# Moving SyncE's jump to its next instruction block from the exit into its idle time before the last store

## Chip, cores and metric

One core of one Trainium2 chip. The metric is the device time of one execution in microseconds (us). Executions are compared as medians of several runs. The profile of one execution has a span of its own, from the first to the last recorded instruction of the program; the device time is about 1.8 us longer than it (1248.58 against 1246.8 for the profiled run before). All times "at 1243.9" are us from the start of the profiled span. Besides the printed views, I use the raw records behind them, which have every instruction with its start and length in ns, every semaphore signal and every DMA packet; tables of SyncE's instructions that are not profile views hold numbers taken from these records.

## The reference

```python
x: (64, 256, 8192) float32
out = np.mean(x, axis=2)          # (64, 256)
```

537 MB are read once and 64 KB are written.

## The kernel before

The 16384 rows are read in 63 blocks of 256 rows (8 MB each) into three buffers. VectorE sums each block. The last 256 rows come in seven smaller loads, so that little is left to do when the last bytes land: row 0 of each partition as one load, row 1 in six chunks of 4096 to 256 columns. SyncE issues all loads and all three stores.

```python
FETCH_BLOCK = 128
LAST_CHUNKS = (4096, 2048, 1024, 512, 256, 256)
# ...
tail_sem = [tc.alloc_semaphore(f"tail{i}") for i in range(len(LAST_CHUNKS) + 1)]

nc.vector.addr_align(FETCH_BLOCK, offset=0, max_nops=0)     # VectorE: at its start, both kernels
# ...
def store_last(r):
    nc.vector.transpose(out=fin_t[r][:], in_=fin[r][:])
    nc.sync.dma_start(out=out_last[r], in_=fin_t[r][0:P:SQ, :])

for n in range(LB):                                   # LB = 63
    xt = slots[n % SLOTS]
    load(xt[:], x_v[n], load_sem[n % LOAD_SEMS])      # issued by SyncE
    # ... VectorE sums it (the last one together with ScalarE)

# ... row 0 of the rest: one load; row 1: one load per chunk, each with its own semaphore;
# ... each but the last is summed by VectorE (the wide ones together with ScalarE)

nc.sync.dma_start(out=out_bulk, in_=bulk[:LB])        # means of the 63 blocks

scaled_sum(fin[0][:, 0:1], head[:])
store_last(0)                                         # row 0
untracked(scaled_sum(fin[1][:, 0:1], fin_in[:, 0 : lastw + k]))._wait_ge(sem, 16)
store_last(1)                                         # row 1: the last store
```

`addr_align(128, max_nops=0)` asks for the next instruction of that engine to be placed at the start of a block of 128 instruction slots, without filling instructions. The trace does not number the slots; it shows the align as one COMPARE_BRANCH (VectorE's at 0.762, 47 ns).

The framework adds the exit, the code that ends every kernel. On SyncE it is three semaphore waits (a semaphore counts signals, in the trace 16 for each load; each of the waits is for one of the three stores, merged with another wait), a drain (DRAIN in the trace), a second drain that signals the barrier, at which each of the five engines waits for the other four (before: SyncE's signal, the last, at 1246.070, and the engines' next instructions between 1246.094 and 1246.226), and the rest of the barrier.

## Time and profile before

| | before |
|---|---|
| device time, median of 3 (lowest to highest) | 1248.35 us (1248.23 to 1248.42) |
| span of the profiled run | 1246.8 us |
| HBM traffic over the span | 431 GB/s |
| last load chunk landed / last store landed | 1242.87 / 1245.43 |
| from the last store's landing to the end of the span | 1.376 us |

From the page of the kernel before: the span, the share of busy DMA and the rate in 40 slices, the DMA queues, and the largest group of instructions (busy us, mean ns | idle us before it and what ended it).

```profile
span 1246.8 us, 224 instructions
...
DMA  9999999999999999999999999999999999999998
GB/s 404 437 437 437 435 431 418 431 437 437 437 437 437 435 433 418 429 437 437 437 437 437 435 431 414 435 437 437 437 437 435 437 429 416 435 437 437 437 437 339
...
q1 hardware_dynamic: 10168, 536.94, 99.6%
q14 instruction: 1, 0.01, 0.0%
...
L95 DVE TENSOR_REDUCE res<-xt 128x2 f32<-128x16384 f32 (+1 forms) x63 | 1076.4, 17086 | 154.0 <-DMA xt<-in_x_dram 154.0
```

The kernel is bound by its loads. DMA is busy nine tenths or more everywhere but in the last slice, and VectorE idles almost only for loads (154.0 us). Queue 14 carries instructions: one packet of 8192 bytes inside the span, at 4.88, 4.1 us after VectorE's jump at 0.76.

The change concerns the last 4 us. The timeline of the kernel before, cut to its end (start us, length us, engine, line, operation):

```profile
1243.19 0.43 DVE L101 TENSOR_SCALAR_CACHE_REDUCE fin_in<-fin_in 128x265 f32<-128x265 f32 x1 [0.15 <-DVE fin_in L95]
1243.55 0.08 DVE L101 DVE_READ_ACCUMULATOR fin_in<-fin_in 128x1 f32 x1
1243.66 0.21 DVE L112 STREAM_TRANSPOSE fin_t<-fin 128x32 f32<-128x32 f32 x1
1243.90 0.50 SPq L113 DMA_DIRECT2D out_dram<-fin_t  x1
```

The timeline ends here, 2.4 us before the span does, because drains and semaphore waits are not counted as work. The view of the exit's source line (L187), cut to the end of the span, has them (duration ns min/median/max, first and last start us):

```profile
L187 SPq EVENT_SEMAPHORE  x5: 17/28/28, 1244.5 to 1246.7; - x5
L187 POOLq EVENT_SEMAPHORE  x4: 17/17/17, 1246.1 to 1246.7; - x4
L187 SPq DRAIN  x3: 7/7/114, 1245.5 to 1246.3; - x3
```

Two of SyncE's drains take 7 ns and one takes 114. The raw records of SyncE show where it stands and what is around it:

```
before           start     ns
last store     1243.902   502   landed 1245.432
wait           1244.450    28
wait           1244.525    28
wait           1245.449    28   (for the last store's landing)
drain          1245.519     7
drain          1245.954   114   signals the barrier at 1246.070
...
end            1246.808
instruction packet, 8192 bytes, at 1246.869
```

Between the starts of the two drains lie 0.435 us; elsewhere in this exit, where nothing has to be awaited, SyncE needs 0.07 to 0.09 us from the start of one instruction to the start of the next. The other four engines had joined the barrier by 1243.93, so everybody waits for this.

### The profile page before, as it was taken

What the parts mean: (1) busy time and instruction counts of PE and PEld (TensorE: products, weight loads), DVE (VectorE), ACT (ScalarE), POOL (GpSimd) and SP (SyncE); (2) the same over time, 40 slices, a digit from 0 to 9 for tenths busy, and PEclk for the clock granted to TensorE, in tenths of its full rate; (3) what the DMA queues carried; (4) which work ended last, traced back from release to release, by engine and by line L of the source; (5) the groups of instructions that cost most, each with busy time, mean ns of one, the idle gap of its engine ahead of it and who ended that gap; (6) DMA issues with size and microseconds to landing.
All of it is one profiled execution on the core that took longest, in us unless ns stands there. A gap on an engine that the chain in (4) does not pass through costs nothing.

```text
span 1246.8 us, 224 instructions
## 1 busy us (share of the span) xinstructions
PE 0.9 (0%) x2; PEld 0.4 (0%) x2; DVE 1087.3 (87%) x79; ACT 16.5 (1%) x13; POOL 0.7 (0%) x6
## 2 busy tenths in 40 slices
PE   0000000000000000000000000000000000000000
PEld 0000000000000000000000000000000000000000
DVE  2898988989889889898898988989889888898897
ACT  0000000000000000000000000000000000000004
POOL 0000000000000000000000000000000000000000
DMA  9999999999999999999999999999999999999998
GB/s 404 437 437 437 435 431 418 431 437 437 437 437 437 435 433 418 429 437 437 437 437 437 435 431 414 435 437 437 437 437 435 437 429 416 435 437 437 437 437 339
DMA packets 10169, 536.95 MB, mean 431 GB/s; under 512 B 1145, under 2 KB 1464, under 8 KB 1720
## 3 DMA queue, kind: packets, MB, share of 16 engines
q1 hardware_dynamic: 10168, 536.94, 99.6%
q14 instruction: 1, 0.01, 0.0%
HBM read 536.87 MB, written 0.07 MB: 431 GB/s over the span
## 4 chain that ended last, share of the span: by engine, by line
DMA 70%; DVE 29%; SPq 0%; issue 0%; DVEq 0%
DMA xt<-in_x_dram 70%; DVE res L95 29%; DVE fin_in L95 0%; SPq L85 0%; DVE fin_in L101 0%; DVE fin_t L112 0%; DVEq L101 0%
## 5 line engine op out<-in xcount | busy, mean ns | idle before, releaser
L95 DVE TENSOR_REDUCE res<-xt 128x2 f32<-128x16384 f32 (+1 forms) x63 | 1076.4, 17086 | 154.0 <-DMA xt<-in_x_dram 154.0
L98 ACT ACT_TABLE_LOAD x1 | 1.3, 1283 | 1182.5 <-DVE res L95 1182.5
L98 ACT ACTIVATE xt<-xt 128x8192 f32<-128x8192 f32 (+5 forms) x6 | 14.7, 2443 | 43.9 <-DMA xt<-in_x_dram 43.7
L95 DVE TENSOR_REDUCE fin_in<-xt 128x1 f32<-128x256 f32 (+3 forms) x5 | 4.9, 1003 | 0.3 <-DMA xt<-in_x_dram 0.2
L95 DVE TENSOR_REDUCE head<-xt 128x1 f32<-128x4096 f32 x1 | 4.4, 4420 | 0.2 <-DMA xt<-in_x_dram 0.2
L154 PE MATMUL ps<-ident,res 128*63 128x128 f32 x2 | 0.9, 458 | 1231.5 <-ACT xt L98 1230.4
L75 DVE MEMSET fin<- 128x32 f32 x2 | 0.1, 85 | 1.4 <-PEq L176 1.4
L98 ACT ACTIVATION_READ_ACCUMULATOR xt<-xt 128x1 f32 x6 | 1.1, 186 | 0.0
L155 DVE TENSOR_SCALAR bulk<-ps 63x128 f32<-63x128 f32 x2 | 0.6, 278 | 0.4 <-PE ps L154 0.4
L154 PEld LDWEIGHTS ps<-ident,res 128*63 128x63 f32 x2 | 0.4, 180 | 1231.8 <-issue 1230.4
L101 DVE TENSOR_SCALAR_CACHE_REDUCE fin_in<-fin_in 128x265 f32<-128x265 f32 x1 | 0.4, 431 | 0.2 <-DVE fin_in L95 0.2
L112 DVE STREAM_TRANSPOSE fin_t<-fin 128x32 f32<-128x32 f32 x2 | 0.4, 211 | 0.1
L63 POOL TENSOR_SCALAR_AFFINE_SELECT ident<-ident 128x128 f32<-128x128 f32 x1 | 0.3, 292 | 0.1
L101 DVE TENSOR_SCALAR_CACHE_REDUCE head<-head 128x2 f32<-128x2 f32 x1 | 0.2, 155 | 0.1
L62 POOL MEMSET ident<- 128x128 f32 x1 | 0.2, 204 | 0.3 <-POOLq L176 0.3
L176 POOL MEMSET const-bfloat16-1.0<- 128x1 bf16 x1 | 0.1, 101 | 0.0
L176 POOL MEMSET const-uint8-127<- 128x1 uint8 x1 | 0.1, 101 | 0.0
L176 POOL MEMSET const-float32-0.0<- 128x1 f32 x1 | 0.1, 98 | 0.2 <-issue 0.2
L176 POOL MEMSET const-float32-1.0<- 128x1 f32 x1 | 0.1, 98 | 0.0
L101 DVE DVE_READ_ACCUMULATOR head<-head 128x1 f32 x1 | 0.1, 83 | 0.0
L101 DVE DVE_READ_ACCUMULATOR fin_in<-fin_in 128x1 f32 x1 | 0.1, 83 | 0.0
## 6 DMA issues: line engine op xcount, KB each, us to landing
xt<-in_x_dram SPq DMA_DIRECT2D x1, 4096.0 KB, 31.1
xt<-in_x_dram SPq DMA_DIRECT2D x1, 2048.0 KB, 35.7
xt<-in_x_dram SPq DMA_DIRECT2D x1, 1024.0 KB, 37.7
xt<-in_x_dram SPq DMA_DIRECT2D x63, 40.8
xt<-in_x_dram SPq DMA_DIRECT2D x1, 512.0 KB, 38.5
xt<-in_x_dram SPq DMA_DIRECT2D x1, 256.0 KB, 38.7
xt<-in_x_dram SPq DMA_DIRECT2D x1, 128.0 KB, 38.5
fin_in<-in_x_dram SPq DMA_DIRECT2D x1, 128.0 KB, 38.4
```

The lines of the kernel that those rows point to most:

```text
L62: nc.gpsimd.memset(ident[:], 0.0)
L63: nc.gpsimd.affine_select(out=ident[:], in_=ident[:], compare_op=mybir.AluOpType.not_equal, fill=1.0, base=0, pattern=[[-1, P]], channel_m ...
L75: nc.vector.memset(fin[r][:], 0.0)
L95: return untracked(nc.vector.tensor_reduce(out=dst, in_=src, axis=X, op=ADD))
L98: return untracked(nc.scalar.activation(out=src, in_=src, func=COPY, accum_out=dst))
L101: return nc.vector.tensor_scalar(out=src, in0=src, scalar1=inv, scalar2=None, op0=mybir.AluOpType.mult, op1=ADD, accum_out=dst,)
L112: nc.vector.transpose(out=fin_t[r][:], in_=fin[r][:])
L154: nc.tensor.transpose(out=ps[:LB, :], in_=res[:, r, :], identity=ident[:])
L155: nc.vector.tensor_scalar_mul(out=bulk[:LB, :, r], in0=ps[:LB, :], scalar1=inv)
L176: nc = _bacc.Bacc("TRN2", target_bir_lowering=False, num_devices=1)
```

## The change

Its intent: I read the hole of 0.435 us as SyncE coming to the end of a block of its instructions in the middle of the exit. It shall go to the next block earlier, at a time when it has nothing to do: after the second-last chunk has landed, while VectorE computes the last sums.

```diff
     def store_last(r):
         nc.vector.transpose(out=fin_t[r][:], in_=fin[r][:])
-        nc.sync.dma_start(out=out_last[r], in_=fin_t[r][0:P:SQ, :])
+        return nc.sync.dma_start(out=out_last[r], in_=fin_t[r][0:P:SQ, :])
@@
     scaled_sum(fin[0][:, 0:1], head[:])
-    store_last(0)
+    st = store_last(0)
+
+    with tc.issue_after(st.ins):
+        st = nc.sync.wait_ge(tail_sem[-2], 16)
+    with tc.issue_after(st.ins):
+        st = nc.sync.addr_align(FETCH_BLOCK, offset=0, max_nops=0)
     untracked(scaled_sum(fin[1][:, 0:1], fin_in[:, 0 : lastw + k]))._wait_ge(sem, 16)
-    store_last(1)
+    with tc.issue_after(st.ins):
+        store_last(1)
```

A comparison of the two built programs shows one instruction more on SyncE (the wait is merged into the align) and the same order on all other engines.

## The prediction

The sum below comes to minus 0.40 us, 1248.35 to 1247.95 us.

> **What bounds the kernel now.** It reads 537 MB once; the page gives 431 GB/s over the 1246.8 us span and DMA nine tenths or more busy in 39 of 40 slices. VectorE (1087 us) waits for loads alone (154 us). The change touches no load and no reduction; it can act only on the last microseconds.

> **The tail, from the raw records of the trace (us from the span's start).** The second-last load chunk has landed at 1242.58, the last at 1242.87. VectorE's last transpose signals at 1243.89. SyncE issues the last store at 1243.90 (0.50 us); it lands at 1245.43. SyncE then passes three semaphore waits (to 1245.48) and a drain (1245.519 to 1245.526). Its next instruction, the drain that joins the exit barrier, starts only at 1245.954 and takes 0.114 us. Elsewhere in this exit SyncE takes 0.07 to 0.09 us from one instruction's start to the next, and its other two drains take 0.007 us (view of the exit's source line). SyncE's waits show this hole as a 0.5 us wait put down to PE, which had long been done. All other engines had joined by 1243.93, so the hole is wholly on the critical path.

> I read it as SyncE stepping into its next instruction block: an 8192-byte packet on the instruction queue follows at 1246.87, 1.3 us later, as one follows VectorE's own jump at 0.76 (at 4.88, behind the first loads). As the fetch comes after the step, the block stepped into was already on the core. [...] this trace shows 8 KiB packets.

> **What the change does.** It adds one SyncE instruction, an align to a 128-instruction block with the wait for the second-last chunk merged into it; nothing moves on the other engines (order compared). SyncE is idle between 1238.55 and 1243.90. The jump starts near 1242.6. VectorE's identical one took some 0.55 us (0.76 to about 1.3), so SyncE is ready at about 1243.2, 0.7 us before the last store is released: off the critical path. Its block fetch (0.31 us on one engine) should run near 1244, between the loads' end (1242.87) and the store's packets (1245.05).

> **Sum.** The hole of 0.435 us between two drains' starts becomes 0.07: minus 0.37. The drain's 0.114 may become 0.01; I count a third of that. About minus 0.40 us: 1248.35 becomes **1247.95 us**, 0.03% less, twice the spread of the runs before (0.19 us). Range for 8 in 10: **1247.70 to 1248.40**. Chances: faster by over 2% 0.002, within 2% 0.996, slower by over 2% 0.002.

> **What would show it right.** SyncE's barrier drain follows the drain before it within 0.1 us; from the store's landing to the span's end falls from 1.37 us to about 0.97; two instruction-queue packets inside the span instead of one; a compare-branch on SyncE near 1242.6; the last store still issues within 0.03 us of the transpose's signal.

> **What would make it wrong.** The target block is not on the core: the jump waits for a fetch, the last store issues late, and the time rises by up to a microsecond. Or the hole is no block step but belongs to the first drain, and stays. Or the fetch collides with the store's packets or descriptors and delays its landing by 0.3 us. Or the shifted code crosses another block after the exit, at the same cost.

## The result

| | before | after |
|---|---|---|
| device time, median of 6 runs (lowest to highest) | 1248.43 us (1248.23 to 1248.86) | 1247.91 us (1247.77 to 1248.15) |
| span of the profiled run | 1246.8 us | 1246.4 us |
| last load chunk landed | 1242.872 | 1242.943 |
| transpose's signal to the last store's issue | 0.016 us | 0.017 us |
| last store's landing to the end of the span | 1.376 us | 0.898 us |

The ratio is 0.9996, with a 95% interval of 0.9983 to 1.0009. Ratios are computed as the mean time of one kernel's runs over that of the other's of the same rounds, so not quite the ratio of the medians quoted. By that interval the kernels are the same within 2%, and it does not by itself exclude no gain. But the slowest run after (1248.15) is faster than the fastest before (1248.23), and the profile shows where the difference lies. Three of the six runs before are those of the first table, and the lines on the tail before come from the profile taken then.

The page after:

```profile
span 1246.4 us, 226 instructions
...
q1 hardware_dynamic: 10168, 536.94, 99.7%
q14 instruction: 2, 0.02, 0.0%
```

There are two packets of instructions in the span instead of one. The timeline after, cut to its end:

```profile
1243.22 0.43 DVE L101 TENSOR_SCALAR_CACHE_REDUCE fin_in<-fin_in 128x265 f32<-128x265 f32 x1 [0.15 <-DVE fin_in L95]
1243.57 0.08 DVE L101 DVE_READ_ACCUMULATOR fin_in<-fin_in 128x1 f32 x1
1243.69 0.21 DVE L112 STREAM_TRANSPOSE fin_t<-fin 128x32 f32<-128x32 f32 x1
1243.93 0.51 SPq L113 DMA_DIRECT2D out_dram<-fin_t  x1
```

The last store follows the transpose as closely as before, so SyncE was back from its jump in time. The views of the align's source line (L164) and of the exit's (now L193):

```profile
L164 SPq NOP  x1: 14/14/14, 1242.6 to 1242.6; - x1
L164 SPq COMPARE_BRANCH  x1: 32/32/32, 1242.7 to 1242.7; - x1
```

```profile
L193 SPq EVENT_SEMAPHORE  x5: 17/28/28, 1244.5 to 1246.3; - x5
L193 SPq DRAIN  x3: 7/7/13, 1245.6 to 1245.9; - x3
```

The drain of 114 ns is gone. In the raw records the hole is gone too:

```
after            start     ns
NOP (the wait) 1242.635    14
COMPARE_BRANCH 1242.697    32
instruction packet, 8192 bytes, at 1243.726, 539 ns
last store     1243.931   512   landed 1245.477
wait           1245.493    28
drain          1245.558    13
drain          1245.628     7   signals the barrier at 1245.637
end            1246.375
```

From the first drain's start to the signal it takes 0.079 us instead of 0.551, which is 0.472 us less. From the store's landing to the end it is 0.478 us less. The device time fell by 0.52 us in the medians. The part ahead of the store's landing varies by some tenths from one execution to the next (the last chunk landed 0.07 us later in the profile after, and between 1242.75 and 1243.15 over all nine profiles), so the stretch after the landing is the cleaner measure, and the table of the experiments uses it.

One of my readings of the profile was wrong. The waits of SyncE before had these lines, of which I took the second for the hole:

```profile
SPq L187 <- DMA out_dram<-fin_t: 0.9, 1, 0.9
SPq L187 <- PEq L187: 0.6, 2, 0.5
```

Both are still there after the change:

```profile
SPq L193 <- DMA out_dram<-fin_t: 0.9, 1, 0.9
...
SPq L193 <- PEq L193: 0.6, 2, 0.5
```

So the second line is something else: SyncE's last wait in the barrier, which begins 0.43 us after the drain ahead of it has ended (1246.313 to 1246.746 before, 1245.880 to 1246.313 after), while GpSimd clears the semaphores (EVENT_SEMAPHORE_RANGE_CLEAR, 142 ns, at 1246.377 before and 1245.943 after). The hole itself is in no view of waits, because SyncE waited for no semaphore in it. Only the starts and lengths of the exit's instructions show it.

### The profile page after: what moved, and what is told of

It is laid out like the page before. It is cut to its first block, busy times and chain, and to the rows that moved or that the text cites. A ratio compares the mean times of both kernels' runs of the same rounds, so it can differ in the third digit from the quotient of the medians.

```text
span 1246.4 us, 226 instructions
## 1 busy us (share of the span) xinstructions
PE 0.9 (0%) x2; PEld 0.4 (0%) x2; DVE 1087.3 (87%) x79; ACT 16.4 (1%) x13; POOL 0.7 (0%) x6
## 4 chain that ended last, share of the span: by engine, by line
DMA 70%; DVE 29%; SPq 0%; issue 0%; DVEq 0%
DMA xt<-in_x_dram 70%; DVE res L95 29%; DVE fin_in L95 0%; SPq L85 0%; DVE fin_in L101 0%; DVE fin_t L112 0%; DVEq L101 0%
```

## The experiments

| run | device time, median (before in the same rounds) | store landed to end of span, us | place of the step |
|---|---|---|---|
| before | 1248.43 (first comparison) | 1.376 | between the drains |
| after | 1247.91 (1248.43) | 0.898 | branch at 1242.7 |
| after_again | 1248.09 (1248.54) | 0.899 | branch at 1242.6 |
| wait_only | 1248.53 (1248.54) | 1.419 | ahead of the first drain |
| shift2 | 1248.03 (1248.54) | 0.930 | among the waits (estimate), no branch |
| late | 1248.17 (1248.54) | 0.898 | branch at 1244.5 |
| early | 1248.11 (1248.45) | 0.893 | branch at 1238.5 |
| twojumps | 1249.46 (1248.45) | 0.887 | branches at 1242.5 and 1243.1 |
| dve_cross | 1248.04 (1248.45) | 0.892 | as after; VectorE's align removed |

Five runs of each, nine of before in each of the two sets (after_again to late on one chip; early, twojumps and dve_cross on another). All gave correct results.

### after_again: the changed kernel beside the others

> The changed kernel again, on the chip of the runs beside it. Both theories expect about 0.5 us less than before (1248.43 to 1247.91 in the first comparison), a compare-branch on SyncE within 0.1 us after the second-last chunk has landed, and no hole at the exit: from the start of SyncE's first exit drain to its signal to the barrier about 0.08 us instead of 0.55.

The branch starts at 1242.641, after the second-last chunk's landing at 1242.563. From the first drain's start (1245.496) to the signal (1245.574) it takes 0.078 us. The medians differ by 0.45 us. The result repeats.

### wait_only: the wait without the align

```diff
     with tc.issue_after(st.ins):
         st = nc.sync.wait_ge(tail_sem[-2], 16)
-    with tc.issue_after(st.ins):
-        st = nc.sync.addr_align(FETCH_BLOCK, offset=0, max_nops=0)
```

> The added wait is kept, the align is taken out: SyncE has one instruction more in the stream, and no jump. Theory (a step into the next block, at a fixed place in the stream): the step now falls one instruction earlier in the exit, ahead of the first exit drain instead of after it, still after the store has landed (1245.4). So the hole of about 0.4 us stays but moves from after that drain to before it; time as before within 0.15 us; one instruction packet inside the span. Rival (the hole belongs to the barrier drain itself, or comes from SyncE having slept since 1238.6 and the added wait wakes it): under the first form the hole stays after the first drain; under the second it is gone and the time falls by 0.5 us as in the changed kernel.

The time is that of before (1248.53 against 1248.54). The exit's drains, in the view of its source line, and the raw records:

```profile
L191 SPq DRAIN  x3: 7/7/112, 1245.8 to 1246.3; - x3
```

```
wait_only        start     ns
wait           1245.358    28
drain          1245.834   112
drain          1246.013     7
```

The long drain is now the first of the three, not the second. The hole moved with it: 0.476 us from the last wait's start to the drain's, where it is 0.065 after the change. So the hole and the slow instruction behind it belong to a place in the stream of instructions and not to a certain drain, and one instruction more shifted them by one. Waking SyncE gains nothing. Both rivals of that kind fall. Only my count of instruction packets was off: the fetch came at 1246.46, just inside the span, so the page counts two.

### shift2: two more instructions and no jump

```diff
-        st = nc.sync.wait_ge(tail_sem[-2], 16)
-    with tc.issue_after(st.ins):
-        st = nc.sync.addr_align(FETCH_BLOCK, offset=0, max_nops=0)
+        st = nc.sync.wait_ge(tail_sem[0], 16)
+    # ... likewise tail_sem[1], tail_sem[2], tail_sem[3]; the four become two instructions
```

> No jump and no align: two wait instructions on chunks that have landed or are about to are put in SyncE's idle time, so everything after them stands two places later. Theory: the step falls between the second and the third semaphore wait of the exit, in the time (1244.55 to 1245.43) in which SyncE waits for the last store to land anyway. It is hidden there: time about 0.45 to 0.5 us below before, equal to the changed kernel within 0.15 us, with no hole among the drains, an instruction packet near 1245.6 to 1245.9 and no compare-branch on SyncE. Rival (the jump itself, or the early fetch, is what helps): no gain, or the hole stays.

The median is 0.51 us below before and 0.06 from the changed kernel's. The drains are quick:

```profile
L197 SPq DRAIN  x3: 7/7/7, 1245.8 to 1246.1; - x3
```

There is no branch on SyncE. The instruction packet comes at 1246.13, somewhat later than I had expected. The place of a hidden step can only be told from its packet. Apart from the run early and the second jump of twojumps, the packet came 1.03 to 1.34 us after SyncE's branch, or after the end of the instruction ahead of the hole, in every profile where that place is known (before: 1245.526 to 1246.869). Reckoned back from 1246.13, that puts the step here, as an estimate, between 1244.79 and 1245.10: after the second wait of the exit, which ends at 1244.786, and well before the store lands at 1245.674. By this estimate the step fell where it was meant to, in the time in which SyncE waits for the store to land. From the landing to the end it takes 0.930 us, 0.03 more than after; this difference lies between the third wait and the first drain (0.099 against 0.065). The branch is not what helps: this shift takes the step off the critical path without one and does the same.

### late: the jump while the store is under way

```diff
-    with tc.issue_after(st.ins):
-        st = nc.sync.wait_ge(tail_sem[-2], 16)
-    with tc.issue_after(st.ins):
-        st = nc.sync.addr_align(FETCH_BLOCK, offset=0, max_nops=0)
 ...
-    with tc.issue_after(st.ins):
-        store_last(1)
+    st = store_last(1)
+    with tc.issue_after(st.ins):
+        nc.sync.addr_align(FETCH_BLOCK, offset=0, max_nops=0)
```

> The align is put after the last store's issue, without a wait, so SyncE jumps at about 1244.45 while the store is under way (landing at about 1245.43). Theory: the jump's 0.5 to 0.6 us end at about 1245.0, before the landing, so it is hidden just as well: about 0.45 us below before, equal to the changed kernel within 0.15 us; the instruction packet runs near 1245.5. Rival (the jump has to come while the sums run, ahead of the last store): gain lost or at most half of it.

The branch starts at 1244.502 and the exit's first wait at 1244.964, so the jump takes 0.46 us. The store lands at 1245.491, and from there to the end it is 0.898 us, exactly as in the changed kernel. The median is 0.37 us below before, with runs from 1247.82 to 1248.54: a little less than I had expected, but the profile has nothing left of the hole, and a difference of 0.08 us to the changed kernel beside it is within the spread of either. The jump need not come while the sums run.

### early: the jump without the wait

```diff
     with tc.issue_after(st.ins):
-        st = nc.sync.wait_ge(tail_sem[-2], 16)
-    with tc.issue_after(st.ins):
         st = nc.sync.addr_align(FETCH_BLOCK, offset=0, max_nops=0)
```

> The changed kernel without its wait: SyncE jumps as soon as the first of the two short stores is issued (1238.6), so the block fetch runs near 1239.7, while loads still stream to 1242.9. The hole at the exit stays away, as in the changed kernel (store's landing to the end 0.90 us). If the fetch takes its 0.3 to 0.5 us from the one queue engine that finishes the loads last, the last chunk lands up to 0.3 to 0.5 us later and most of the gain is lost; if it falls to any other engine the time equals the changed kernel's within 0.15 us. There the wait for the second-last chunk is only a precaution.

The branch runs at 1238.541, but the instruction packet only at 1241.602, 3.06 us later, where the changed kernel needed 1.03. There the last load had landed 0.78 us before the packet ran; here, as at VectorE's packet at the start (4.1 us after its jump), loads were under way. What held these two packets back was not shown. The packet runs before the loads are done, and yet the last chunk landed at 1242.804, no later than in the other profiles (1242.75 to 1243.15), and the last of its 16 completion signals was 0.60 us behind the one before it, against 0.77 in the last chunk that landed before the fetch. No delay of the loads shows. The exit is as good (0.893 us). The median is 0.34 us below before, against 0.45 and 0.52 for the changed kernel in other rounds and 0.41 for dve_cross, which has the wait, in the same rounds. So the wait was worth about 0.1 us or nothing; five runs do not settle which.

### twojumps: a second jump right behind the first

```diff
     with tc.issue_after(st.ins):
         st = nc.sync.addr_align(FETCH_BLOCK, offset=0, max_nops=0)
+    # ... three satisfied waits on tail_sem[0], [1], [2]
+    with tc.issue_after(st.ins):
+        st = nc.sync.addr_align(FETCH_BLOCK, offset=0, max_nops=0)
```

> The changed kernel with a second align after the first, two satisfied waits between them, so that SyncE jumps twice: into the block that is on the core, and from there at once into the one behind it, whose fetch only the first jump sets off (it ran from 1.05 us after the branch, for 0.5 us). If a block that is not on the core has to be awaited, the second jump, near 1243.1, ends only after that fetch has landed near 1244.2, the last store issues 0.4 to 1.0 us late, and the time is 0.4 to 1.0 us above the changed kernel, that is at or above the time before. If two blocks ahead are already held, the second jump ends near 1243.6, in time for the store at 1243.9, and the time equals the changed kernel's within 0.15 us.

The expectation spoke of two waits between the aligns. There are three in the program; in the trace two of them are one instruction, and the third is merged into the second align. The timeline of this run, cut to its end:

```profile
1243.51 0.21 DVE L112 STREAM_TRANSPOSE fin_t<-fin 128x32 f32<-128x32 f32 x1
1245.31 0.52 SPq L113 DMA_DIRECT2D out_dram<-fin_t  x1
```

The store issues 1.58 us after the transpose's signal (1243.733 to 1245.309), although it waited for no other semaphore. The first branch took 0.451 us (1242.521 to the next instruction at 1242.972); the second took 2.18 us (1243.127 to 1245.309). The time is 1.01 us above before and so about 1.5 us above the changed kernel. The direction is as the expectation has it for a block that is not on the core: SyncE goes on only after the packet that followed the first jump, 2.79 us after that jump. The size was more than I had expected (0.4 to 1.0 us). The packet ran from 1243.798 to 1244.122, and SyncE went on 1.19 us after that. What it did in this time no record shows. When SyncE has gone on, the next packet follows at 1245.887.

This is the failure that the prediction named first. The changed kernel has one jump alone; such a first jump took 0.45 us here and 0.46 in late, and not 2.18, and here SyncE went on from it 0.83 us before the packet ran. So what it went on with was already on the core.

### dve_cross: VectorE without its align

```diff
-    nc.vector.addr_align(FETCH_BLOCK, offset=0, max_nops=0)
```

> The changed kernel without the align at VectorE's start, which both kernels have. The theory that a step into the next block sits at a fixed place in each engine's stream, if VectorE starts its stream about where SyncE does, puts VectorE's step some 4 instructions ahead of its last drain: a hole of about 0.4 us at the last wait, the last sum or the last transpose, on the critical path. Against that, no fetch of VectorE runs at 5 us among the first loads, so if that fetch sets one DMA engine 0.31 us behind for good, the last chunk lands up to 0.3 us earlier. Sum: 0.1 to 0.5 us above the changed kernel. If there is no hole on VectorE and no earlier landing, the time equals the changed kernel's.

My expectation was wrong in its place: VectorE does not step just ahead of its last drain, so by the theory it does not start its stream where SyncE does. There is no hole in the tail, and the time equals the changed kernel's (0.41 us below before). The branch of VectorE and the packet near 5 us are gone. In their place one packet runs in the middle of the run, so I take it that VectorE's step is now there; no hole of VectorE shows it, as VectorE waits for a load before each sum (2.13 to 2.84 us in these lines). The timeline there (in brackets: VectorE's idle time before the instruction):

```profile
816.21 17.22 DVE L94 TENSOR_REDUCE res<-xt 128x2 f32<-128x16384 f32 x1 [2.13 <-DMA xt<-in_x_dram]
835.55 17.22 DVE L94 TENSOR_REDUCE res<-xt 128x2 f32<-128x16384 f32 x1 [2.13 <-DMA xt<-in_x_dram]
855.62 17.22 DVE L94 TENSOR_REDUCE res<-xt 128x2 f32<-128x16384 f32 x1 [2.84 <-DMA xt<-in_x_dram]
874.96 17.22 DVE L94 TENSOR_REDUCE res<-xt 128x2 f32<-128x16384 f32 x1 [2.13 <-DMA xt<-in_x_dram]
```

The only instruction packet among the loads runs at 839.638, for 0.33 us. The next block lands 0.71 us late, once. In the raw records each load ends with 16 signals. Up to that packet the last of them comes about 0.13 us after the one before it, and from then on, for the 400 us to the end, about 0.7 us after it. With the align at the start the first load bears this instead: it lands at 22.67 here and at 23.12 to 23.44 in the other profiles. So at both of these places one fetch of 8 KB set the loads behind it back by 0.45 to 0.77 us. It is no rule for every place: in early a fetch ran at 1241.602 among the last loads and the last chunk was not late. Both kernels have VectorE's fetch among the loads once (at 4.88 before, 5.08 after). SyncE's fetch holds up no load in either, since it comes after the last one (at 1246.869 against 1242.872 before, 1243.726 against 1242.943 after).

This run also shows what VectorE's own jump costs: its first MEMSET starts at 0.814 us here and at 1.35 to 1.38 us behind the branch in the other profiles, 0.53 to 0.57 us later.

A kernel without a fetch among the loads might gain as much as the change did; this is an estimate from the 0.45 to 0.77 us, and no run tests it. I found no cheap way to it: the packet here runs during the 47th of VectorE's 87 recorded instructions, so the step can't be put behind the last load without taking almost half of its work away. No variant tried beats the changed kernel.

## Why the prediction was right

The time on record was 1247.95 us; measured were 1247.91. The mechanism held as far as the runs show it, but that the two agree to 0.04 us is in part luck. The prediction took 0.40 us off 1248.35, while the median before was 1248.43 in the comparison and the drop 0.52; the runs after are themselves 0.38 us apart. The fair comparison is 0.40 us predicted for the tail against 0.48 measured there. Point by point:

- **The hole is on the critical path and is a block step.** Shown is that it belongs to a place in the stream: it moves by one instruction in wait_only, vanishes among the waits in shift2, and the device time follows both times (1248.53 and 1248.03 against 1248.54). That a block begins there is my reading of the 8192-byte packet that follows. The changed kernel lost 0.45 and 0.52 us in two comparisons.
- **"The hole of 0.435 us between two drains' starts becomes 0.07".** It became 0.070 (1245.558 to 1245.628).
- **"The drain's 0.114 may become 0.01; I count a third of that".** This term was mis-sized. The drain became 0.007, so the whole 0.107 us belongs to the step, not a third (0.036). wait_only shows it: there the long drain (112 ns) is the one next behind the step. From the last store's landing to the end the prediction had 0.97 us, and 0.898 was measured. The whole step costs 0.47 us in the profile, not 0.40 (0.52 in that of wait_only: 1.419 against 0.898).
- **The jump is hidden.** The prediction took VectorE's 0.55 us (0.53 to 0.57 by dve_cross) and 0.7 us of slack. SyncE's own jump takes 0.45 to 0.46 (late, twojumps), and the store issued 0.017 us after its signal.
- **The block is on the core.** Shown by the contrast within twojumps: SyncE went on 0.45 us after the first jump, 0.83 us before the packet ran, and 2.18 us after the second, 1.19 us after the packet had ended.
- **The fetch collides with nothing.** It ran at 1243.73 for 0.54 us, longer than the 0.31 expected but between the last load and the store's packets. The store's landing took 1.55 us from its issue, against 1.53 before: not the 0.3 us later that the prediction feared.
- **The reading of the waits** as another view of the hole was wrong, as told with the result. Nothing in the sum rested on it.

## What to carry to other kernels

In these runs SyncE stood still for about half a microsecond where, as I read it, it stepped or jumped into its next block of instructions (0.45 to 0.52 us), and VectorE at its jump likewise (0.53 to 0.57); the place of SyncE's step moved with the number of instructions put ahead of it (wait_only, shift2). When a kernel is otherwise at its limit, look for a gap of 0.4 us between two instructions that wait for nothing, above all in the tail and at the exit. One or two extra instructions, or an align put into idle time, moved it off the critical path here (0.34 to 0.52 us in the medians); but a second jump 0.6 us after the first took 2.18 us (twojumps). Measure such a gain on a stretch of the profile that begins behind the noise (here the last store's landing), since in the device time of single runs it is barely larger than their spread.
